# Hybrid encoder on one core: the roundings of the first part's operand sums one pair later, and the loads of the running sums spread over blocks 9 to 13

## The chip, the core and the metric

The kernel runs on one core of one Trainium2 chip. The metric is the device time of one execution, in microseconds: the median of the runs. The compute engines are PE (TensorE, matmuls, with PEld for its weight loads), DVE (VectorE), ACT (ScalarE) and POOL (GpSimd). DMAs are issued from the queues of SP (SyncE) and POOL.

## The reference, cut to what matters

Two layers (`DEPTH = 2`) on 512 tokens of width 1024, all in float32. Each layer mixes tokens in three ways, and then comes a SwiGLU feed-forward network (FFN), which the change is in:

```python
h = rmsnorm(x, norm_ffn[i])
x = x + (jax.nn.silu(h @ w_ffn_gate[i]) * (h @ w_ffn_up[i])) @ w_ffn_down[i]
```

`w_ffn_gate` and `w_ffn_up` are 1024 x 2816, `w_ffn_down` is 2816 x 1024. A per-layer input embedding follows, and a final norm behind the second layer.

## The kernel before, in words

**Operands in two halves.** A float32 operand is split in a high half (rounded to fp32r by ACT) and a low half (the difference, by DVE): `split`, lines 169 to 171, whose two instructions stand at lines 150 (ACT) and 164 (DVE) in the profile, as do all that go through the helpers `act` and `tt`. A product of two operands is three matmuls: high by high, high by low, low by high. In `seven` they are lines 1135, 1136 and 1137.

**The FFN in blocks and parts.** `ffn` walks over the 2816 inner columns in 22 blocks of 128, in three parts: blocks 0 to 7, 8 to 14 and 15 to 21 (`PARTS`). For each block `seven` computes gate and up together by a scheme of seven half-sized products in place of eight (of the Strassen kind): PE runs, in this order, a11·b11 into PSUM tile A, a22·t4 into Q, s2·t1 into C ("five"), a12·b21 onto A, s1·t3 onto Q, s3·t2 into A's other half, s4·b22 into C. Each is twelve matmuls of 128 x 256. The s are sums of weights, the t are sums of activations. Even blocks use the PSUM tags `mm`, odd blocks `sc`, `sc`, `av`.

ACT copies the products p1 (A, before a12·b21 is added onto it), p4 (Q, before s1·t3 is added) and p5 ("five") to SBUF; the products that add onto A and Q wait for these copies. p1 and p4 are the two halves of one tile of tag `t` (`ffn_t` in the profile), p5 is a tile of tag `a`. DVE then combines: p4 − p5, gate's two halves `gg` (scaled by the norm's factor `rb`), p1's difference, up's two halves `uu`. The first instruction that writes the tile `uu` is `uu0`, p1's difference minus Q.

**What follows a block.** `rest` (silu of `gg` on ACT, the product with `uu` on DVE, the split of the block's result into `md`) is kept in `self.pending`; `flush` runs it in the middle of the next block, right behind that block's copy of p5. At its end `rest` calls `done`.

**Pairs of blocks.** The first part's down product is again of the seven-product kind (`seven_down`, four calls, lines 1008 to 1088), in steps of pairs of blocks: (0, 1), (2, 3), (4, 5), with blocks 6 and 7 taken whole. It needs four sums t1 to t4 for each pair. `done` of the odd block calls `middles` (lines 996 to 1006), which makes them in two float32 tiles of tag `t` (DVE, 128 x 256 each) and right away splits each of them: four roundings on ACT, four low halves on DVE. The targets lie in tiles of tag `x`, in unused halves of `md`, and for the pair (2, 3) in tiles of the FFN's input.

**The running sums.** `seven_down` adds nothing to the residual: its eight results go to a DRAM buffer `xa` (line 1088, `xa<-ffn_t`) and come back as the tiles `x[m]` (line 1254, `ffn_x<-xa`), which the later parts' down products add to. Part 1 reads them first, behind block 14.

**Weights.** Each block loads its gate and up weights by four DMAs of SP (`ffn_qk<-w_fg`, `ffn_qk<-w_fu`, `ffn_wr<-w_fg`, `ffn_r<-w_fu`) and two accumulating ones of POOL; ACT rounds them and DVE makes their low halves and the sums s3 and s4. The order between the last: low half of a22 (`ffn_a<-ffn_r,ffn_kh`), then s3 (`ffn_qk<-ffn_qk,ffn_r`), then s4 (`ffn_qk<-ffn_qk,ffn_wr`), then the rounding of both (`ffn_pt` or `ffn_y`). `ffn_r` comes free when s3 is done.

**What sets the order.** PE's order is that of the code (`manual_schedule`). All other engines, and the queues of SP and POOL, are ordered by the framework's planner: it goes by priority, which is the place in the code (weights count as 400 instructions earlier, `w_ahead`), and places an instruction when its inputs are ready by its own durations. Buffers of a tag are handed out in the code order of first writes, so a tile's first write is not placed ahead of the first write of a tile of the same tag that comes earlier in the code: p1's copy of block n+1 not ahead of `uu0` of block n (tag `t`, seven buffers); the low half of a later block's a22 not ahead of the next block's copy of p5 (tag `a`, three buffers).

Of the kernel before, what the change touches and what calls it, by code (L numbers as in the profile page):

```python
# [26 lines left out]
KD = 8  # L27
# [41 lines left out]
class Net:  # L69
# [926 lines left out]
    def middles(self, at, even, odd):  # L996

        u, w = self.sb("t", [P, 2, 256]), self.sb("t", [P, 2, 256])
        t1, t2, t3, t4 = u[:, 0], u[:, 1], w[:, 0], w[:, 1]
        self.tt(t1, even[:, 0], even[:, 1], ALU.subtract)  # L1000
        self.tt(t2, odd[:, 1], t1, ALU.add)
        self.tt(t3, odd[:, 1], even[:, 1], ALU.subtract)
        self.tt(t4, odd[:, 0], t2, ALU.subtract)
        for (hi, lo), t in zip(at, (t1, t2, t3, t4)):
            self.split(hi, lo, t)
        return {f"t{n + 1}": t for n, t in enumerate(at)}

    def seven_down(self, p, w0, w1, bs, late, spare):

# [195 lines left out]
    def ffn(self, h, x):  # L1205
        self.phase = "ffn"
        i = self.i
        self.halfs, self.pending = 0, []
        nc, st, hn, bs = self.nc, [], [], self.four
        spare = [[self.sb(t, [P, 1024], F32R) for _ in range(2)] for t in ("pt", "y")]  # L1210
        md8 = [self.sb(t, [P, 2, 512], F32R) for t in ["v"] * 3 + ["z"] + ["y"] * 3]
        md8.append(tuple(self.sb("e", [P, 512], F32R) for _ in range(2)))
        low, xt = [], []
        for n in range(4):
            t = self.sb("x", [P, 2, 512], F32 if n == 2 else F32R)
            if n == 2:
                xg = t
            else:
                xt.append([(t[:, u, :256], t[:, u, 256:]) for u in range(2)])
        self.sums, self.sevens = [t for _ in range(2) for t in self.parts_of("qk", [1024], 2)], 0  # L1220
        for part in PARTS:
            mids = []
            for f, fb in enumerate(part):
                tags = (("mm", "mm", "mm"), ("sc", "sc", "av"))[fb % 2]
                md = md8[f]
                mids.append(md)
                wg, wu = self.a["w_fg"][i, fb], self.a["w_fu"][i, fb]
                gg = xg[:, fb // 2 % 2].rearrange("p (a b) -> p a b", a=2) if fb in (0, 2, 4) else None

                def done(gg, fb=fb):  # L1230
                    if fb > 5:
                        return
                    ha = self.halves(md8[fb - fb % 2])
                    cut = lambda p, c: (p[0][:, c], p[1][:, c])
                    one, two = slice(0, 256), slice(256, 512)
                    own = [cut(ha, two)]
                    if fb % 2 == 0:
                        self.even = gg
                    else:
                        hb = self.halves(md8[fb])  # L1240
                        at = (xt[0] + xt[1][:1] + own, [cut(self.halves(t), two) for t in h[::2]],
                              xt[1][1:] + xt[2] + own)[fb // 2]
                        low.append(dict(b11=cut(ha, one), b21=cut(hb, one), b22=cut(hb, two),
                                        **self.middles(at, self.even, gg)))

                self.seven(wg, wu, bs, tags, spare[fb % 2], md, part[0] and f < 2, fb, gg, done)
            self.flush()
            if part is PARTS[0]:
                for p in range(4):
                    w0, w1 = (self.a["w_fd"][i, 2 * p + u] for u in range(2))  # L1250
                    self.seven_down(p, w0, w1, low, mids[6:], spare[p % 2])
                x[:] = [t for _ in range(KD // 2) for t in self.parts_of("x", [512], 2)]
                for m in range(KD):
                    nc.sync.dma_start(x[m], self.xa[m])
                continue
            down = [self.a["w_fd"][i, m][:, part[0] * P:(part[-1] + 1) * P] for m in range(KD)]
            end = part is PARTS[-1]
            afresh = AFRESH[PARTS.index(part)]
            xs = [x[m] if m >= afresh else self.sb("a", [P, 512]) for m in range(KD) if end]
            for m in range(afresh if end else 0):  # L1260
                nc.sync.dma_start(xs[m], self.xp[m])
            two = [self.ps(("mm", "sc")[fb % 2 == 0]) for _ in range(2)]
            self.pair(two, down[:2], mids)
            for m in range(KD):
                if m < 2:
                    ps = two[m]
                else:
                    ps = self.ps("mm")
                    if m >= afresh:
                        self.act(ps, x[m], AF.Copy)  # L1270
                        if end:
                            nc.sync.dma_start(xs[m], self.xp[m])
                    self.gemm(ps, down[m], mids, m >= afresh)
                if not end and m >= afresh:
                    self.act(x[m], ps, AF.Copy)
                    continue
                if not end:
                    self.tt(x[m], x[m], ps, ALU.add)
                    continue
                d = self.sb("t", [P, 512])  # L1280
                if m < afresh:
                    self.tt(d, x[m], ps, ALU.add)
                    ps = d
                self.tt(d, ps, self.rb, ALU.mult)
                self.tt(x[m], xs[m], d, ALU.add)
                if m in (0, 2):
                    qk = self.parts_of("qk", [2, 512], 2, F32R)
                hn.append(self.norm_chunk(m, x[m], self.par(i, "ple", m),
                                          qk[m % 2] if m < 4 else "z", st))
        self.main_norm(st[0])  # L1290
        return hn
# [352 lines left out]
```

## Time and profile before

| | |
|---|---|
| median of 3 runs | 1772.17 us (1770.05 to 1772.83) |
| the profiled execution | 1771.02 us |
| its span in the profile | 1769.2 us |
| granted TensorE clock | 0.999 |
| DMA | 275.50 MB, 156 GB/s on average |
| the first part's blocks 3 to 7, layer 0 | 523.21 to 576.29 us |
| the first part's down product, layer 0 | 576.29 to 617.53 us |
| block 9, layer 0 | 627.57 to 638.46 us |

How to read it: a line of a timeline gives start and duration in microseconds, engine, line, operation, the tiles written and read (`out<-in`), and in brackets how long the engine stood before it and which instruction released it. `L150` and `L164` are the helpers, so instructions are told apart by their tiles. A tile's name is its phase and its tag: `ffn_t` is any tile of tag `t` in the FFN. A matmul's duration is longer than its distance to the next, as matmuls overlap; waits of PE are read from start to start. In a table of windows each engine has its busy time and, in brackets, its number of instructions.

### The profile page before, as it was taken

The numbers are of one execution on the slowest core, as the hardware profiler recorded it, in microseconds if no ns is written. First come the engines' busy times: TensorE is split into PE (matmuls) and PEld (weight loads), VectorE is DVE, ScalarE is ACT, GpSimd is POOL, SyncE is SP. The second block draws the span as 40 slices with busy tenths as digits, with TensorE's granted clock in tenths as the row PEclk, the third lists the DMA queues.
The fourth block names the chain that finished last, engine by engine and source line by source line (L and its number), as shares of the span: only waits on it lengthen the run. The fifth ranks groups of instructions, "written<-read, shape, count | busy, mean of one in ns | idle before, by whom it ended". The sixth has DMA issues, their size and how long they took to land.

```text
span 1769.2 us, 27985 instructions
## 1 busy us (share of the span) xinstructions
PE 1756.1 (99%) x10362; PEld 1559.0 (88%) x10362; DVE 1430.5 (81%) x2434; ACT 915.7 (52%) x1599; POOL 112.3 (6%) x130
## 2 busy tenths in 40 slices
PE   9999999999999999999999999999999999999998
PEld 7888888888899999998888888888888999989987
DVE  7967988998899886687777688889887997866776
ACT  5576555325566454454545665552356554534454
POOL 0000000000111111100000000000001111101000
PEclk9999999999999999999999999999999999999999
DMA  6576641334867886545546755323358678755342
GB/s 227 161 187 158 160 125 54 102 99 151 258 164 168 225 220 160 136 124 163 164 135 171 184 151 153 106 76 92 107 182 236 167 166 241 211 143 152 99 152 95
DMA packets 127529, 275.50 MB, mean 156 GB/s; under 512 B 16032, under 2 KB 31136, under 8 KB 127392
## 3 DMA queue, kind: packets, MB, share of 16 engines
q1 hardware_dynamic: 111696, 246.19, 45.7%
q0 software_dynamic: 14976, 26.22, 9.3%
q8 instruction: 81, 1.33, 0.3%
q10 hardware_dynamic: 720, 1.31, 0.2%
q14 instruction: 56, 0.46, 0.1%
HBM read 227.52 MB, written 15.73 MB: 137 GB/s over the span
## 4 chain that ended last, share of the span: by engine, by line
PE 92%; DVE 3%; DMA 2%; ACT 2%; issue 1%; POOL 0%; SPq 0%; ACTq 0%; POOLq 0%; DVEq 0%
PE ffn_mm L1135 4%; PE ffn_mm L1137 4%; PE ffn_mm L1136 4%; PE ffn_sc L1137 3%; PE ffn_sc L1135 3%; PE ffn_sc L1136 3%; PE ffn_mm L185 3%; PE ffn_mm L186 3%; PE ffn_mm L187 3%; PE mergea_mm L185 2%; PE mergea_mm L187 2%; PE mergea_mm L186 2%; PE gateb_mm L187 2%; PE gateb_mm L186 2%; PE gateb_mm L185 2%; PE wo_mm L187 2%
## 5 line engine op out<-in xcount | busy, mean ns | idle before, releaser
L167 DVE SCALAR_TENSOR_TENSOR conv_z<-glu_z,pre_par,conv_z 128x512 f32<-128x512 f32 x240 | 179.4, 747 | 3.5
L150 ACT ACTIVATE ffn_wh<-ffn_wr 128x1024 fp32r<-128x1024 f32 (+1 forms) x84 | 84.5, 1010 | 63.4 <-PE ffn_mm L186 32.4
L164 DVE TENSOR_TENSOR ffn_wl<-ffn_wr,ffn_wh 128x1024 fp32r<-128x1024 f32 (+1 forms) x84 | 97.8, 1169 | 21.3 <-ACT ffn_wh L150 20.8
L1105 POOL DMA_DIRECT2D ffn_qk<-w_fu x88 | 77.9, 980 | 525.6 <-DMA ffn_qk<-w_fu 236.2
L150 ACT ACTIVATE ffn_wh<-ffn_qk 128x1024 fp32r<-128x1024 f32 x52 | 55.1, 1060 | 44.4 <-PE ffn_mm L1061 17.8
L164 DVE TENSOR_TENSOR ffn_wl<-ffn_qk,ffn_wh 128x1024 fp32r<-128x1024 f32 x52 | 63.6, 1223 | 16.9 <-ACT ffn_wh L150 16.6
L150 ACT ACTIVATE mergea_wh<-mergea_wr 128x1024 fp32r<-128x1024 f32 (+1 forms) x32 | 27.1, 846 | 96.8 <-PE mergea_mm L186 79.6
L164 DVE TENSOR_TENSOR ffn_t<-ffn_t,ffn_t 128x512 f32<-128x512 f32 (+1 forms) x58 | 34.6, 596 | 25.4 <-ACT ffn_t L150 24.8
L150 ACT ACTIVATE ffn_kh<-ffn_r 128x512 fp32r<-128x512 f32 (+1 forms) x52 | 31.9, 613 | 42.1 <-DMA ffn_r<-w_fu 12.7
L150 ACT ACTIVATE natten_e<-natten_e,natten_s 128x192 f32<-128x192 f32 (+1 forms) x88 | 39.3, 473 | 25.1 <-DVE natten_s L732 21.8
L1135 PE MATMUL ffn_sc<-wo_h,ffn_wh 128*128 128x256 f32 x176 | 50.0, 284 | 1.5 <-ACT ffn_t L150 1.5
L150 ACT ACTIVATE diff_a<-diff_sc,diff_s 128x512 f32<-128x512 f32 x32 | 22.0, 686 | 56.8 <-DVE diff_s L925 56.7
L1137 PE MATMUL ffn_mm<-wo_h,ffn_wl 128*128 128x256 f32 x176 | 49.8, 283 | 0.0
L1136 PE MATMUL ffn_mm<-wo_h,ffn_wh 128*128 128x256 f32 x176 | 49.8, 283 | 0.0
L1136 PE MATMUL ffn_sc<-wo_h,ffn_wh 128*128 128x256 f32 x176 | 49.8, 283 | 0.0
L1135 PE MATMUL ffn_mm<-wo_h,ffn_wh 128*128 128x256 f32 x176 | 49.8, 283 | 0.0
L1137 PE MATMUL ffn_sc<-wo_h,ffn_wl 128*128 128x256 f32 x176 | 49.8, 283 | 0.0
L231 POOL TENSOR_TENSOR diff_rc<-diff_sm,pre_power 128x4 f32<-128x4 f32 x8 | 8.9, 1115 | 563.0 <-DVE diff_sm L167 504.4
L164 DVE TENSOR_TENSOR diff_wl<-diff_wr,diff_wh 128x1024 fp32r<-128x1024 f32 x24 | 29.3, 1223 | 18.7 <-ACT diff_wh L150 13.6
L150 ACT ACTIVATE natten_wh<-natten_wr 128x1024 fp32r<-128x1024 f32 x24 | 25.4, 1059 | 36.7 <-issue 15.2
L925 DVE TENSOR_REDUCE diff_s<-diff_sc 128x1 f32<-128x512 f32 x64 | 42.0, 682 | 2.2 <-PE diff_sc L834 2.1
L164 DVE TENSOR_TENSOR natten_wl<-natten_wr,natten_wh 128x1024 fp32r<-128x1024 f32 x24 | 29.3, 1222 | 12.3 <-ACT natten_wh L150 10.4
(1086 smaller groups left out, 6817.3 us busy)
## 6 DMA issues: line engine op xcount, KB each, us to landing
ffn_qk<-w_fu POOLq DMA_DIRECT2D x88, 256.0 KB, 6.1
ffn_wr<-w_fg SPq DMA_DIRECT2D x44, 512.0 KB, 5.1
ffn_wr<-w_fd SPq DMA_DIRECT2D x32, 448.0 KB, 4.0
ffn_r<-w_fu SPq DMA_DIRECT2D x44, 256.0 KB, 3.8
ffn_qk<-w_fg SPq DMA_DIRECT2D x44, 256.0 KB, 5.3
ffn_qk<-w_fu SPq DMA_DIRECT2D x44, 256.0 KB, 5.4
natten_wr<-w_in SPq DMA_DIRECT2D x16, 512.0 KB, 4.4
diff_wr<-w_in SPq DMA_DIRECT2D x16, 512.0 KB, 4.0
```

What stands on the lines that cost most here:

```text
L150: i = self.nc.scalar.activation(out, in_, func, **kw)
L164: return self.nc.vector.tensor_tensor(out, a, b, op)
L167: return self.nc.vector.scalar_tensor_tensor(out, a, s, b, op0, op1)
L185: mm(out, wh, ah, start=first, stop=False, skip_group_check=onto)
L186: mm(out, wh, al, start=False, stop=False, skip_group_check=onto)
L187: mm(out, wl, ah, start=False, stop=last, skip_group_check=onto)
L231: nc.gpsimd.tensor_tensor(col, ms, self.power, ALU.pow)
L925: nc.vector.tensor_reduce(out=m[:, u:u + 1], in_=sc, op=ALU.max, axis=AX.X, negate=True)
L1105: nc.gpsimd.dma_start(q, wu[:, lo], accum_op=ALU.add)
L1135: mm(out, wh[:, c], bh, start=first and k == 0, stop=False, skip_group_check=True)
L1136: mm(out, wh[:, c], bl, start=False, stop=False, skip_group_check=True)
L1137: mm(out, wl[:, c], bh, start=False, stop=k == 3, skip_group_check=True)
```

## The change

`middles` no longer splits the four sums. It puts target and sum in a list, `self.parted`, and a new method `part_sums` splits all that the list holds. `done` of an even block calls it: so the sums of pair (0, 1), made in `done` of block 1, are split in `done` of block 2, those of pair (2, 3) in `done` of block 4, those of pair (4, 5) in `done` of block 6 (for blocks 6 and 7 `done` does nothing else). In the code each group of splits thus comes one block later, and the two tiles of sums are held a block longer.

The eight loads of the running sums no longer stand together behind the first part. They stand ahead of blocks of the second part: sum 0 ahead of block 9, 1 ahead of 10, 2 and 3 ahead of 11, 4 and 5 ahead of 12, 6 and 7 ahead of 13. The number of instructions is the same.

```diff
@@ middles @@
-        for (hi, lo), t in zip(at, (t1, t2, t3, t4)):
+        self.parted += zip(at, (t1, t2, t3, t4))
+        return {f"t{n + 1}": t for n, t in enumerate(at)}
+
+    def part_sums(self):
+
+        for (hi, lo), t in self.parted:
             self.split(hi, lo, t)
-        return {f"t{n + 1}": t for n, t in enumerate(at)}
+        self.parted = []
@@ ffn @@
-        low, xt = [], []
+        low, xt, self.parted = [], [], []
...
             for f, fb in enumerate(part):
+                for m in {9: (0,), 10: (1,), 11: (2, 3), 12: (4, 5), 13: (6, 7)}.get(fb, ()):
+                    nc.sync.dma_start(x[m], self.xa[m])
...
                 def done(gg, fb=fb):
                     if fb > 5:
-                        return
+                        return self.part_sums()
...
                     if fb % 2 == 0:
+                        self.part_sums()
                         self.even = gg
...
                 x[:] = [t for _ in range(KD // 2) for t in self.parts_of("x", [512], 2)]
-                for m in range(KD):
-                    nc.sync.dma_start(x[m], self.xa[m])
                 continue
```

## The prediction

> **What bounds the kernel now.** I read the page first, then the waits of PE, then PE's timeline at each wait, the windows of the blocks around it, and last the timelines of ACT, DVE and SP in those windows.
>
> ```profile
> span 1769.2 us, 27985 instructions
> PE 1756.1 (99%) x10362; PEld 1559.0 (88%) x10362; DVE 1430.5 (81%) x2434; ACT 915.7 (52%) x1599; POOL 112.3 (6%) x130
> ```
>
> TensorE is busy for 1756.1 of 1769.2 us. The change takes no matmul away, so all it can give is time in which PE stands. PE's waits, and the matmuls that end three of them, in the first layer:
>
> ```profile
> PE ffn_av L1135 <- ACT ffn_t L150: 3.9, 4, 1.6
> PE ffn_sc L1135 <- ACT ffn_t L150: 1.5, 2, 0.7
> ```
> ```profile
> 528.42 0.39 PE L1135 MATMUL ffn_sc<-wo_h,ffn_wh 128*128 128x256 f32 x1 [0.75 <-ACT ffn_t L150]
> 531.73 0.38 PE L1135 MATMUL ffn_av<-wo_v,ffn_wh 128*128 128x256 f32 x1 [1.62 <-ACT ffn_t L150]
> 634.06 0.39 PE L1135 MATMUL ffn_av<-wo_v,ffn_wh 128*128 128x256 f32 x1 [0.60 <-ACT ffn_t L150]
> ```
>
> The two largest waits are PE waiting for ACT to copy p1 and p4 out of PSUM, in block 3 (528.42, 531.73) and block 9 (634.06). The windows show each block whole; the columns are length, then busy time of PE, PEld, DVE, ACT, POOL, clock, DMA share and GB/s. The first five are blocks 3 to 7 of layer 0, then block 9, then blocks 3 and 9 of layer 1.
>
> ```profile
> 523.21:536.13 12.92, 10.55 (x86) 10.15 (x85) 12.91 (x26) 6.90 (x14) 1.76 (x2) 1.00 0.73 200
> 536.13:546.17 10.04, 10.04 (x86) 10.04 (x85) 8.71 (x17) 5.98 (x10) 1.76 (x2) 1.00 0.71 173
> 546.17:556.22 10.05, 10.05 (x87) 10.05 (x86) 9.96 (x20) 6.24 (x11) 1.75 (x2) 1.00 0.69 156
> 556.22:566.25 10.03, 10.03 (x86) 10.03 (x85) 9.97 (x19) 6.19 (x11) 1.79 (x2) 1.00 0.71 175
> 566.25:576.29 10.04, 10.04 (x86) 10.04 (x85) 10.01 (x22) 5.87 (x11) 1.72 (x2) 1.00 0.68 155
> 627.57:638.46 10.89, 10.29 (x87) 10.09 (x86) 7.28 (x14) 5.45 (x9) 1.78 (x2) 1.00 0.78 235
> 1398.93:1411.70 12.77, 10.56 (x86) 10.16 (x85) 12.76 (x26) 6.63 (x13) 1.75 (x2) 1.00 0.67 189
> 1503.14:1513.67 10.53, 10.32 (x86) 10.12 (x85) 7.30 (x14) 5.45 (x9) 1.75 (x2) 1.00 0.79 229
> ```
>
> An undisturbed block lasts 10.04. Block 3 costs 2.88 and 2.73 over that in the two layers, 5.61 together; block 9 costs 0.85 and 0.49, together 1.34. Those 6.95 us are the most that the change can give. In block 3 DVE has no gap (12.91 of 12.92) and in blocks 5 to 7 hardly one; in block 4 it has 1.33 idle.
>
> **Part 1, the low halves of the sums.** ACT in block 3, then in block 5, which has no stall:
>
> ```profile
> 527.70 0.38 ACT L150 ACTIVATE ffn_a<-ffn_sc 128x256 f32<-128x256 f32 x1 [0.62 <-PE ffn_sc L1137]
> 527.98 0.38 ACT L150 ACTIVATE ffn_t<-ffn_sc 128x256 f32<-128x256 f32 x1
> 530.35 1.06 ACT L150 ACTIVATE ffn_pt<-ffn_qk 128x1024 fp32r<-128x1024 f32 x1 [1.99 <-DVE ffn_qk L164]
> 531.32 0.36 ACT L150 ACTIVATE ffn_t<-ffn_av 128x256 f32<-128x256 f32 x1
> ```
> ```profile
> 549.66 0.36 ACT L150 ACTIVATE ffn_t<-ffn_sc 128x256 f32<-128x256 f32 x1
> 550.67 0.38 ACT L150 ACTIVATE ffn_a<-ffn_sc 128x256 f32<-128x256 f32 x1 [0.38 <-PE ffn_sc L1137]
> ```
>
> In block 5 ACT copies p1 (549.66), then p4, then p5 (550.67). In block 3 the order is p5, p1, the rounding of s3 and s4 (`ffn_pt`), p4; both waits follow from it. ACT idles 0.62 ahead of p5, so p1 is not late for lack of ACT: its place in the queue is wrong. The planner hands out a tag's buffers in code order of first write, so p1's buffer of block n+1 comes behind `uu` of block n, which DVE writes first in `uu0` (p1 minus Q). If DVE reaches `uu0` only when p5 is ready, p5 goes first. So: `uu0` must start before p5 of the next block.
>
> What holds `uu0` up in block 3 is four low halves of the sums (columns: start, duration), while the `uu0` of blocks 3 to 6, which run in blocks 4 to 7, stand here with them:
>
> ```profile
> 526.03 1.09 DVE L164 TENSOR_TENSOR ffn_x<-ffn_t,ffn_x 128x256 fp32r<-128x256 f32 x3
> 527.04 0.42 DVE L164 TENSOR_TENSOR ffn_v<-ffn_t,ffn_v 128x256 fp32r<-128x256 f32 x1
> 537.07 0.42 DVE L164 TENSOR_TENSOR ffn_t<-ffn_t,ffn_av 128x256 f32<-128x256 f32 x1
> 550.19 0.42 DVE L164 TENSOR_TENSOR ffn_t<-ffn_t,ffn_mm 128x256 f32<-128x256 f32 x1
> 558.94 0.42 DVE L164 TENSOR_TENSOR ffn_t<-ffn_t,ffn_av 128x256 f32<-128x256 f32 x1
> 570.61 0.42 DVE L164 TENSOR_TENSOR ffn_t<-ffn_t,ffn_mm 128x256 f32<-128x256 f32 x1
> ```
>
> Three low halves take 526.03 to 527.04, 0.336 each from start to start; four take 1.35. Behind them stand p4−p5, a product and p1's difference at the same step, three more, so `uu0` of block 2 could start at 526.03 + 3 × 0.336 = 527.04 instead of behind s3 and s4, 0.66 ahead of p5 at 527.70. Then p1 and p4 are copied first, as in block 5, and both waits go: −5.61 over the two layers. The low halves and ACT's four roundings are not saved, only moved; ACT is half idle (6.90 of 12.92) and hides its share at no cost, but if DVE's cover is gone each low half costs up to 0.336.
>
> What is late next? Without the stall DVE loses 2.88 us per layer in which it caught up. Its work in blocks 3 to 7 is 12.91 + 8.71 + 9.96 + 9.97 + 10.01 = 51.56, less 1.36 of the last pair's low halves, which move behind block 7: 50.2, in 5 × 10.04 = 50.2. No slack. I carry the debt on. p5 is copied 4.50 into a block (550.67 − 546.17).
> - Block 4: `uu0` at 537.07 − 536.13 = 0.94, plus 2.88 of debt (the first pair's low halves now lie ahead of it): 3.82, margin 0.68.
> - Block 5: the debt falls by block 4's 1.33 to 1.55, and this pair's 1.36 lies behind: 4.02 + 0.19 = 4.21, margin 0.29.
> - Block 6: 558.94 − 556.22 = 2.72, plus 1.55: 4.27, margin 0.23.
> - Block 7: 570.61 − 566.25 = 4.36, plus 0.19: 4.55, 0.05 too late; but the next low half of the weights (tag `a`, as p5) is handed its buffer only behind p5, so DVE has nothing to put ahead of `uu0`, and p1 slips by one copy at most.
>
> So a slip in block 7 costs the first of block 3's two waits, 0.75, not the second. The next step is the down product; ACT's row gives what a 128x512 tile takes there.
>
> ```profile
> 578.10 0.28 PE L1049 MATMUL ffn_tr<-ffn_x,ffn_pt 128*128 128x256 f32 x1
> 584.39 0.41 PE L1061 MATMUL ffn_mm<-ffn_e,ffn_wh 128*128 128x512 f32 x1
> ```
> ```profile
> 576.83 0.68 DVE L164 TENSOR_TENSOR ffn_t<-ffn_t,ffn_t 128x512 f32<-128x512 f32 x1
> 579.82 0.42 DVE L164 TENSOR_TENSOR ffn_t<-ffn_t,wo_rb 128x256 f32<-128x256 f32 x1
> 580.89 0.42 DVE L164 TENSOR_TENSOR ffn_a<-ffn_tr,ffn_t 128x256 f32<-128x256 f32 x1 [0.65 <-PE ffn_tr L1051]
> 583.56 0.68 DVE L164 TENSOR_TENSOR ffn_e<-ffn_t,ffn_e 128x512 fp32r<-128x512 f32 x1
> ```
> ```profile
> 633.11 0.63 ACT L150 ACTIVATE ffn_kh<-ffn_r 128x512 fp32r<-128x512 f32 x1 [3.52 <-DMA ffn_r<-w_fu]
> ```
>
> Block 7's own low half ends at 583.56 + 0.68 = 584.24, 0.15 ahead of its use at 584.39; PE will be there 2.88 sooner, at 581.51. Block 7's last result ends at 579.82 + 0.42 = 580.24; DVE can make up at most block 4's 1.33 and some 0.19 in the gaps of blocks 5 to 7, so that becomes 578.72 or later. From there silu, product, rounding and low half take between 2.62 (0.63 + 0.68 + 0.63 + 0.68, back to back) and 4.00 (as now): 581.34 to 582.72. PE waits between nothing and 1.21. I take 0.6, the middle, because both ends have DVE rows behind them (the 0.65 idle at 580.24 can be filled): +1.2 for two layers. A slip in block 7 hands its 0.75 to DVE and takes the place of this wait, so the two are not added.
>
> **Part 2, the loads of the running sums.** SP at the last stores, the release of the buffer that its next load needs, and what waits:
>
> ```profile
> 588.83 0.33 SPq L1254 DMA_DIRECT2D ffn_x<-xa  x1
> 619.26 0.92 SPq L1088 DMA_DIRECT2D xa<-ffn_t  x2
> 624.84 1.11 SPq L1254 DMA_DIRECT2D ffn_x<-xa  x2
> 626.06 0.44 SPq L1103 DMA_DIRECT2D ffn_r<-w_fu  x1
> ```
> ```profile
> 620.35 0.68 DVE L164 TENSOR_TENSOR ffn_qk<-ffn_qk,ffn_r 128x512 f32<-128x512 f32 x1
> ```
> ```profile
> 771.67 0.33 SPq L842 DMA_DIRECT2D diff_r<-rope  x1
> ```
>
> SP stands until the stores of 619.26 have landed (5.58), loads the last two sums at 624.84, and only then issues `ffn_r` at 626.06, whose buffer was free at 621.03. `ffn_r` lands before 633.11 (the ACT row above); ACT stands 3.52 for it with p4's copy behind it, and that is block 9's wait. The change writes these loads later in the code. But the planner issues a load when its inputs and buffer are ready: the rope tables of layer 1 went at 771.67, before half of the span (884.6), about where layer 1 begins, and the first sum at 588.83, right after its store. The two last loads stay where they become ready, so I count nothing. If `ffn_r` does pass them it comes up to 5 us sooner (626.06 − 621.03) and the whole 1.34 goes. A loss is left out: the sums are first read in part 1's down product, five blocks on. Ends: 0 and −1.34; I take 0.
>
> By the Trainium skill ("DMA: Bandwidth & Descriptors", section "Anatomy of one DMA"), whose fit stands for the GpSimd path, a transfer takes about 2.0 us plus its bytes over 436 GB/s, most of the fixed part being the receipt of the write. An estimate by it for one 256 KB store is 2.6 us, so SP would be free some 3 us sooner and block 9 would not wait at all; the trace has 5.58, so it does not agree here, and by the page part 2 would be worth nothing even if the loads moved.
>
> **Sum.** −5.61 + 1.2 + 0 = −4.4: 1766.6 for the profiled execution (1771.02), and, as that lies 1.15 below the median of 1772.17, 1767.8 for the median. A measurement of this kernel tells from no change about 0.2%, 3.5 us.
>
> **Rivals.**
> - Both parts work: −5.61 + 1.2 − 1.34 = −5.75, 1766.4; without the wait for block 7's low half −6.95, 1765.2. For it: `ffn_r` stands in the queue behind loads that nobody needs before part 1's down product. Against it: 771.67. Chance 0.15.
> - The stall only moves or shrinks. With margins of 0.2 to 0.7, a few tenths of difference between the planner's durations and the trace's turn the order again in one of blocks 4 to 7, with up to 2.88 per layer: nothing left. Or block 3 keeps its order and only the second wait shrinks by 1.35: −2.7, 1769.5. Between 1769 and 1772.5; chance 0.26.
> - The change does nothing: the planner fills DVE as before and leaves the low halves where they were: 1772.2. Against it: they now rank behind block 2's results. Chance 0.06.
> - Slower: the last pair's low halves come too late. The down product reads the second of them at 578.10, in the new time 575.2; the product of block 6 at 576.83 ranks ahead of them and becomes 574.1 (1.36 + 1.36 earlier); two low halves behind it end at about 575.5, some 0.1 late, which is within the 0.6 taken above. From there each 0.1 us costs 0.2 over two layers; above 2.8 late the gain is used up. Behind block 7's last result (580.24 − 2.7 + 0.8 = 578.3) they are 3.1 late, +0.6, 1772.8; behind its low half (584.24) 7.1 late, +8.6, 1780.8. Against it: by rank they stand ahead of all of block 7's results. Chance 0.11, of which 0.07 is slower by over 0.2%.
>
> **How the numbers follow.** The forecast has 0.42. Of it 0.36 lies beyond 3.5 us of gain, the rest (a wait at its upper end) within; with the first rival faster has 0.51. Within 0.2%: 0.06 + 0.26 + 0.06 + 0.04 = 0.42; slower 0.07. The range goes from 1765.2 to 1772.8, which leaves out the slow end and the executions' own scatter.
>
> **What would show it.** In the changed profile: block 3 at 10.04 in both layers with p1, p4, p5 in ACT's queue in that order (right), or p5 first again (wrong); the first pair's four low halves behind `uu0` of block 2; no block of 4 to 7 above 10.1 except block 7 by up to 0.75; a wait of PE L1061 for DVE `ffn_e` of 0 to 1.2; block 9 still 10.89 and 10.53, with the last loads of sums issued ahead of `ffn_r`. The forecast is wrong if one of blocks 4 to 7 shows a wait above 1 us, if L1049 waits for `ffn_x`, or if block 9 falls to 10.04.

## The result, and the profile after

The changed kernel takes 1764.93 us (median of 6 runs, 1763.43 to 1765.64), the kernel before, timed beside it, 1771.58 (6 runs, 1769.46 to 1772.83): a ratio of 0.9963, with a 95% interval of 0.9950 to 0.9976, so 6.65 us less (4.3 to 8.9). The forecast was 1767.8, from 1765.2 to 1772.8: the sign is right, and the median lies 0.27 us below the lower end. The page of the changed kernel:

```profile
span 1763.0 us, 27985 instructions
PE 1754.5 (100%) x10362; PEld 1557.8 (88%) x10362; DVE 1429.8 (81%) x2434; ACT 915.8 (52%) x1599; POOL 112.4 (6%) x130
```

Its profiled execution took 1764.80. The waits of PE (line numbers from `seven` on are five higher than before), then the windows of blocks 3, 4, 7 and 9 of layer 0 and of blocks 3 and 9 of layer 1, then the down product of layer 0:

```profile
PE ffn_av L1140 <- ACT ffn_t L150: 1.4, 2, 0.8
```
```profile
522.22:532.26 10.04, 10.04 (x86) 10.04 (x85) 10.04 (x20) 6.55 (x13) 1.77 (x2) 1.00 0.72 192
532.26:542.30 10.04, 10.04 (x86) 10.04 (x85) 10.01 (x19) 5.46 (x9) 1.77 (x2) 1.00 0.70 169
562.38:572.42 10.04, 10.04 (x86) 10.04 (x85) 10.04 (x22) 6.58 (x13) 1.72 (x2) 1.00 0.66 181
623.84:634.66 10.82, 10.28 (x86) 10.08 (x85) 7.27 (x14) 5.45 (x9) 1.78 (x2) 1.00 0.79 226
1395.14:1405.18 10.04, 10.04 (x86) 10.04 (x85) 9.96 (x20) 6.27 (x12) 1.75 (x2) 1.00 0.68 181
1496.75:1507.88 11.13, 10.30 (x87) 10.10 (x86) 7.29 (x14) 5.45 (x9) 1.75 (x2) 1.00 0.76 220
```
```profile
572.42:613.80 41.38, 41.38 (x303) 39.17 (x301) 33.52 (x60) 17.04 (x22) 7.05 (x8) 1.00 0.81 223
```

Block 3 lasts 10.04 in both layers: its 2.88 and 2.73 are gone. The wait on p1 (`ffn_sc`) has left the list, and of the wait on p4 (`ffn_av`) only block 9's is left. Blocks 4 to 7 are at 10.04, with DVE full in each (10.01 to 10.04). No wait for the last pair's sums (`ffn_x`) is in the list: of their four low halves the last two run at 573.42 and 573.76, in time. Block 9 still waits, in layer 1 even more (11.13). ACT in block 3:

```profile
526.01 0.37 ACT L150 ACTIVATE ffn_t<-ffn_sc 128x256 f32<-128x256 f32 x1
526.27 0.38 ACT L150 ACTIVATE ffn_t<-ffn_av 128x256 f32<-128x256 f32 x1
526.72 0.39 ACT L150 ACTIVATE ffn_a<-ffn_sc 128x256 f32<-128x256 f32 x1
```

p1, p4, p5: the order of the blocks without a stall.

### The profile page after: what moved, and what is told of

The parts are those of the page before. It is cut to its first block, busy times and chain, and to the rows that moved or that the text cites. A ratio compares the mean times of both kernels' runs of the same rounds, so it can differ in the third digit from the quotient of the medians.

```text
span 1763.0 us, 27985 instructions
## 1 busy us (share of the span) xinstructions
PE 1754.5 (100%) x10362; PEld 1557.8 (88%) x10362; DVE 1429.8 (81%) x2434; ACT 915.8 (52%) x1599; POOL 112.4 (6%) x130
## 3 DMA queue, kind: packets, MB, share of 16 engines
q8 instruction: 81, 1.33, 0.3%
## 4 chain that ended last, share of the span: by engine, by line
PE 97%; DMA 1%; ACT 1%; DVE 1%; issue 0%; POOL 0%; ACTq 0%; POOLq 0%; DVEq 0%
PE ffn_mm L1140 4%; PE ffn_mm L1142 4%; PE ffn_mm L1141 4%; PE ffn_sc L1142 3%; PE ffn_sc L1140 3%; PE ffn_sc L1141 3%; PE ffn_mm L187 3%; PE ffn_mm L186 3%; PE ffn_mm L185 3%; PE mergea_mm L187 2%; PE mergea_mm L186 2%; PE mergea_mm L185 2%; PE diff_sc L834 2%; PE diff_mm L185 2%; PE diff_mm L187 2%; PE gatec_mm L186 2%
```

## The experiments

The theory: PE waited because p1 stood behind p5, and p4 behind the rounding of s3 and s4 too, in ACT's queue, and they stood there because DVE came to `uu0` too late. The rival: the time that DVE (or ACT) spends on the split is itself what PE waited for, so that any work moved out of block 3 gives its time. Beside them, the loads of the running sums may have given a part.

Each run is one edit to the kernel before or after. The runs of the kernel before that stand beside them have medians of 1770.22 to 1770.87 (19 to 25 runs), so runs of different sets are compared by their ratios to them.

**The roundings and low halves alone** (the kernel after, with the loads back where they were).

```diff
-                for m in {9: (0,), 10: (1,), 11: (2, 3), 12: (4, 5), 13: (6, 7)}.get(fb, ()):
-                    nc.sync.dma_start(x[m], self.xa[m])
...
+                for m in range(KD):
+                    nc.sync.dma_start(x[m], self.xa[m])
```

> Only the roundings and low halves of the sums move; the loads of the running sums stay in one place behind the first part. If the whole gain comes from block 3 (the order of ACT's copies), this is as fast as the full change: 1765 us, block 3 at 10.04 in both layers, block 9 still above 10.4. If the loads gave part of the gain (the measured 6.65 us are more than the 5.4 that block 3 lost between the two traces), this is slower than the full change: 1766 or more, with the difference in block 9 or behind it.

Measured: 1765.22, ratio 0.9969 (0.9958 to 0.9981), which can't be told from the full change. Block 3 is at 10.04 in both layers.

```profile
523.95:533.99 10.04, 10.04 (x87) 10.04 (x85) 10.04 (x20) 6.55 (x13) 1.76 (x2) 1.00 0.77 213
```

Within the intervals the whole gain comes from this part. Block 9 fell to 10.47 and 10.04 without its loads having moved, the first sign that its wait scatters.

**The loads alone** (the opposite edit, to the kernel before).

> Only the loads of the running sums move in the code. If the planner issues a load when it is ready, SP's order and everything else is that of the kernel before: 1771.6 us within 0.1%, block 3 at 12.9 and 12.8, block 9 within its scatter. If the place in the code counts, ffn_r passes the loads and block 9 falls to 10.04: 1.3 us less, 1770.2.

Measured: 1770.72, ratio 1.0001 (0.9992 to 1.0010). SP issues the last loads between the stores and `ffn_r`, as before; every engine and every queue has the order of the kernel before, instruction by instruction:

```profile
619.83 0.92 SPq L1088 DMA_DIRECT2D xa<-ffn_t  x2
624.88 0.93 SPq L1225 DMA_DIRECT2D ffn_x<-xa  x2
625.91 0.44 SPq L1103 DMA_DIRECT2D ffn_r<-w_fu  x1
```

Moving these eight loads in the code as the change does has no effect.

**p1 and p4 in a tag of their own** (to the kernel before; the low halves stay where they were).

```diff
-        o = self.sb("t", [P, 2, 256])
+        o = self.sb("o", [P, 2, 256], bufs=2)
...
-        self.bufs = dict(wr=3, wh=3, wl=3, h=8, qk=2, kh=2, v=4, pt=2, y=5, z=5, x=4, t=7, rp=4,
-                         e=4, a=3, r=2, rb=1, ss=1, sm=8, rc=4, b=2, s=8)
+        self.bufs = dict(wr=3, wh=3, wl=3, h=8, qk=2, kh=2, v=4, pt=2, y=5, z=5, x=4, t=6, rp=4,
+                         e=4, a=3, r=2, rb=1, ss=1, sm=8, rc=3, b=2, s=8)
```

> The kernel before, with the low halves where they were, but p1 and p4 in a tag of their own (two buffers; tag t has six in place of seven and a small tag three in place of four), so that their place in ACT's queue no longer hangs on uu0. If the order of ACT's copies is the cause, block 3 falls to 10.04 in both layers though the four low halves still stand ahead of uu0, and the time is 1766 (5.4 less). If the time that DVE spends on the low halves is the cause by itself, block 3 stays at 12.9 and the time at 1771.6. With one buffer of tag t less, another wait may appear elsewhere; then block 3 alone decides.

Measured: 1766.29, ratio 0.9977 (0.9967 to 0.9987), with block 3 at 10.04 in both layers. Block 3 of both layers, then ACT's copies and DVE's low halves and `uu0` in it:

```profile
524.33:534.37 10.04, 10.04 (x87) 10.04 (x86) 10.04 (x19) 5.85 (x11) 1.77 (x2) 1.00 0.75 179
1396.81:1406.85 10.04, 10.04 (x86) 10.04 (x85) 10.04 (x19) 5.86 (x11) 1.76 (x2) 1.00 0.61 171
```
```profile
525.97 0.38 ACT L150 ACTIVATE ffn_o<-ffn_sc 128x256 f32<-128x256 f32 x1 [1.51 <-PE ffn_sc L1137]
527.95 0.37 ACT L150 ACTIVATE ffn_o<-ffn_av 128x256 f32<-128x256 f32 x1
528.83 0.38 ACT L150 ACTIVATE ffn_a<-ffn_sc 128x256 f32<-128x256 f32 x1 [0.51 <-PE ffn_sc L1137]
```
```profile
526.99 1.08 DVE L164 TENSOR_TENSOR ffn_x<-ffn_t,ffn_x 128x256 fp32r<-128x256 f32 x3
531.13 0.41 DVE L164 TENSOR_TENSOR ffn_t<-ffn_o,ffn_mm 128x256 f32<-128x256 f32 x1
```

This is the run that decides between the two theories: the low halves stand where they stood, `uu0` comes at 531.13, 2.3 us behind p5, and PE does not wait, because p1 (525.97) and p4 no longer hang on it. What PE waited for was the place of two copies in ACT's queue; DVE's time mattered only in that the planner placed p1 by it. About 1 us is lost elsewhere: block 0 lasts 11.39 and 11.38 against 10.89 and 10.88 before, and in it `wo_tr` waits for POOL's `wo_rc`, whose tag has one buffer less (0.6 in total).

**The last loads behind `ffn_r`** (to the kernel after).

```diff
-            nc.sync.dma_start(a22, wu[:, up])
+            self.rl[fb] = nc.sync.dma_start(a22, wu[:, up])
...
-                    nc.sync.dma_start(x[m], self.xa[m])
+                    load = nc.sync.dma_start(x[m], self.xa[m])
+                    if m > 5:
+                        self.behind(load, self.rl[11])
```

> The full change, and the last two loads of running sums are put behind the ffn_r of block 11 in SP's queue. If those loads held ffn_r up (SP stood 5.6 us for the stores, its buffer was free after 1.8), ffn_r is issued some 3 to 4 us sooner, block 9 falls from 10.9 and 11.0 to 10.04 in the two layers and the time by 1.8 us, to 1763. If the transfer itself is late whatever its place (7.8 us from its issue to ACT's rounding), block 9 keeps half of its wait or more: 1764 to 1765.

Measured: 1764.35, ratio 0.9964 (0.9952 to 0.9977). SP after the last stores, first of the change, then of this run, and block 9 of both layers in this run:

```profile
615.52 0.93 SPq L1093 DMA_DIRECT2D xa<-ffn_t  x2
620.50 0.91 SPq L1230 DMA_DIRECT2D ffn_x<-xa  x2
621.52 0.44 SPq L1108 DMA_DIRECT2D ffn_r<-w_fu  x1
```
```profile
616.87 0.92 SPq L1093 DMA_DIRECT2D xa<-ffn_t  x2
618.70 0.33 SPq L1108 DMA_DIRECT2D ffn_r<-w_fu  x1
```
```profile
625.18:635.22 10.04, 10.04 (x87) 10.04 (x85) 8.08 (x15) 5.67 (x9) 1.78 (x2) 1.00 0.82 236
1497.35:1507.39 10.04, 10.04 (x86) 10.04 (x85) 8.08 (x15) 5.67 (x9) 1.76 (x2) 1.00 0.91 223
```

`ffn_r` is issued 1.83 behind the stores in place of 6.00, and block 9 is at 10.04 in both layers. That the new order brought this is not shown: in the eleven profiles with the old order in SP's queue, 7 of the 22 blocks 9 have no wait to speak of (0.05 or less) either, in the run with p1 and p4 in a tag of their own those of both layers. The time does not fall by the 1.8 expected; it can't be told from the change's. With the old order block 9's wait is 0.85 and 0.49 in the kernel before, 0.43 and nothing with the low halves alone, nothing and 1.52 in the run that follows, on average over the eleven profiles some 0.9 for both layers together: that is what there is to gain, and it is below what these runs resolve.

**Only the first pair later** (to the kernel after, with the loads back where they were; the other pairs are split at once).

```diff
-    def middles(self, at, even, odd):
+    def middles(self, at, even, odd, low):
...
         self.parted += zip(at, (t1, t2, t3, t4))
+        if len(low):
+            self.part_sums()
```

> Only pair (0, 1) is split a block later; pairs (2, 3) and (4, 5) are split at once, as before, and the loads stand where they were. If what counts is where uu0 stands against p5 in each block, block 3 falls to 10.04, and the stall comes back in block 5, where pair (2, 3)'s low halves still stand ahead of uu0 and DVE now carries a debt of some 1.3 us: 0.75 to 2.9 per layer, so 1766.5 to 1770.5. If only the low halves in block 3 matter, this is as fast as moving all three pairs: 1765, and no block from 4 to 7 is longer than 10.1.

Measured: 1771.14, ratio 1.0004 (0.9994 to 1.0013): nothing is gained. Blocks 3 and 5 of layer 0 (block 5 of layer 1 lasts 13.27), and ACT in block 5:

```profile
523.24:533.28 10.04, 10.04 (x86) 10.04 (x85) 10.04 (x20) 6.54 (x13) 1.77 (x2) 1.00 0.73 179
543.32:556.32 13.00, 10.57 (x86) 10.16 (x85) 12.98 (x27) 7.37 (x14) 1.76 (x2) 1.00 0.65 180
```
```profile
547.82 0.38 ACT L150 ACTIVATE ffn_a<-ffn_sc 128x256 f32<-128x256 f32 x1 [0.61 <-PE ffn_sc L1144]
548.10 0.38 ACT L150 ACTIVATE ffn_t<-ffn_sc 128x256 f32<-128x256 f32 x1
550.53 1.06 ACT L150 ACTIVATE ffn_pt<-ffn_qk 128x1024 fp32r<-128x1024 f32 x1 [2.05 <-DVE ffn_qk L164]
551.49 0.37 ACT L150 ACTIVATE ffn_t<-ffn_av 128x256 f32<-128x256 f32 x1
```

The stall has moved to block 5, line for line the picture of block 3 before: p5, p1, the rounding of s3 and s4, p4. The stall, 2.96 and 3.23, is a little above the range expected. Moving block 3's low halves is not enough; the later pairs must move as well.

**Roundings at once, low halves later** (all pairs, to the kernel after with the loads back where they were; one run).

```diff
+        for (hi, lo), t in self.parted:
+            self.act(hi, t, AF.Copy)
...
-            self.split(hi, lo, t)
+            self.tt(lo, t, hi.bitcast(F32), ALU.subtract)
```

> All three pairs: ACT rounds the sums at once, as before, and only DVE's low halves come a block later; the loads stand where they were. If DVE's place in time is all that counts, as fast as the full change: 1765, block 3 at 10.04. If ACT's four roundings (0.4 us each) also hold p1 or p4 up, block 3 keeps a wait of some tenths.

Measured: 1765.43, block 3 at 10.04 in both layers. ACT's roundings play no part in block 3's stall; a single time says no more.

**The first pair's low halves twice** (to the kernel after: the same result is written a second time).

```diff
             self.split(hi, lo, t)
+            if self.more:
+                self.tt(lo, t, hi.bitcast(F32), ALU.subtract)
+        self.more = self.more and not self.parted
```

`self.more` is true at the start of each `ffn`, so only the first group of sums is written twice.

> The full change, with each low half of pair (0, 1) computed twice: 4 times 0.336 = 1.35 us more for DVE per layer, in block 4 ahead of uu0 of block 3. That uu0 started 3.74 into block 4 with p5 at 4.50, so the margin of 0.76 is exceeded. If the order theory holds, p5 goes first in block 4, and PE waits there for p1 and perhaps p4: 0.75 to 2.9 per layer, 1766.4 to 1770.7. If DVE's total work is what counts, block 4 stays at 10.04 and the 1.35 arrive at the low half of block 7's result in the down product: 0.7 to 1.3 per layer there, 1766.4 to 1767.6.

Measured: 1770.16, ratio 0.9998 (0.9988 to 1.0007). Block 4 of layer 0 (in layer 1 it lasts 12.74):

```profile
533.52:546.23 12.71, 10.54 (x86) 10.14 (x85) 12.71 (x25) 6.15 (x10) 1.77 (x2) 1.00 0.76 207
```

1.35 us of DVE work bring 2.7 us of stall back in each layer, in the block whose margin they exceed.

**One low half twice** (to the kernel after).

```diff
-        for (hi, lo), t in self.parted:
+        for n, ((hi, lo), t) in enumerate(self.parted):
             self.split(hi, lo, t)
+            if self.more and n < 1:
+                self.tt(lo, t, hi.bitcast(F32), ALU.subtract)
+        self.more = self.more and not self.parted
```

> The full change, with only one low half of pair (0, 1) computed twice: 0.336 us more for DVE per layer. In the full change uu0 of block 3 started 3.74 into block 4 and uu0 of block 4 started 4.22 into block 5, with p5 at 4.50. If the margins decide, block 4 keeps its order (3.74 + 0.34 = 4.08) and block 5 loses it (4.22 + 0.34 = 4.56): p5 goes first there and PE waits 2.5 to 3 us per layer, so one instruction of 0.42 us in each layer costs 5 to 6 us: 1770 to 1771. If the time lost grows with the work added, it costs at most 0.34 per layer, 1765.6.

Measured: 1766.69, ratio 0.9978 (0.9968 to 0.9987). By the ratios that is 1.6 us above the low halves alone and 2.7 above the change, less than the intervals can tell; the traces give 1.01 per layer. Blocks 4 and 5 of layer 0, then ACT in block 5:

```profile
533.45:543.49 10.04, 10.04 (x87) 10.04 (x85) 10.01 (x20) 5.58 (x9) 1.76 (x2) 1.00 0.74 197
543.49:554.54 11.05, 10.30 (x87) 10.10 (x86) 11.05 (x22) 6.90 (x13) 1.75 (x2) 1.00 0.71 194
```
```profile
547.99 0.38 ACT L150 ACTIVATE ffn_a<-ffn_sc 128x256 f32<-128x256 f32 x1 [0.61 <-PE ffn_sc L1145]
548.27 0.38 ACT L150 ACTIVATE ffn_t<-ffn_sc 128x256 f32<-128x256 f32 x1
548.53 0.39 ACT L150 ACTIVATE ffn_t<-ffn_av 128x256 f32<-128x256 f32 x1
```

The place was right, block 5 and not block 4, and one instruction of 0.42 us costs 1.01 in each layer (block 5 of layer 1 is 11.05 too). The price was wrong, 2.5 to 3 were expected: a narrow miss puts only p5 ahead of p1, and p4 keeps its place, so only the first of the two waits comes back.

**The first pair's low halves twice, with the own tag** (both edits shown above, to the kernel after).

> All four low halves of pair (0, 1) twice (1.35 us more per layer, as in the run that brought the stall back in block 4), and p1 and p4 in a tag of their own, so that their place in ACT's queue does not hang on uu0. If the stall in block 4 was the order, blocks 4 and 5 stay at 10.04 and only the debt is paid, at the low half of block 7's result in the down product: 0.9 to 1.35 per layer; with the 1.1 that the own tag's smaller buffers cost beside, 1768 to 1769. If DVE's added work makes the stall by itself, block 4 waits 2.6 per layer again and the time is 1770 or more.

Measured: 1768.39, ratio 0.9987 (0.9978 to 0.9997). Block 4 and the down product:

```profile
534.25:544.29 10.04, 10.04 (x86) 10.04 (x85) 10.04 (x20) 5.00 (x8) 1.76 (x2) 1.00 0.72 190
574.41:617.45 43.04, 41.75 (x302) 39.16 (x301) 35.20 (x66) 17.57 (x23) 7.07 (x8) 1.00 0.80 219
```

Blocks 4 to 7 stay at 10.04; the debt is paid once, in the down product: 43.04 against 41.50 with the own tag alone, 1.54 (43.06 and 1.56 in layer 1) and so a little above the range expected, which ended at 1.35. The 0.2 between is not explained. The stall of the run without the own tag was the order.

**The last pair's low halves twice** (to the kernel after).

```diff
             self.split(hi, lo, t)
+            if self.last:
+                self.tt(lo, t, hi.bitcast(F32), ALU.subtract)
...
+                        self.last = True
                         return self.part_sums()
```

> The full change, with each low half of pair (4, 5) computed twice: 1.35 us more for DVE per layer, behind block 7's uu0 test, so the order of ACT's copies stays. In the changed kernel the low half of block 7's result ended at 580.51, with its use at about 580.5: no margin. The extra 1.35 then reach it, less what the chain behind block 7's last result has in pauses (3.28 used against 2.62 back to back): a wait of 0.7 to 1.35 per layer at the whole products of the down product, 1766.3 to 1767.6. If that low half still has slack of its own, nothing: 1765.

Measured: 1767.86, ratio 0.9983 (0.9974 to 0.9992). The whole products of the down product, and its window:

```profile
581.10 0.49 PE L1067 MATMUL ffn_mm<-ffn_e,ffn_wh 128*128 128x512 f32 x1 [0.39 <-ACT ffn_e L150]
581.84 0.50 PE L1068 MATMUL ffn_mm<-ffn_e,ffn_wh 128*128 128x512 f32 x1 [0.24 <-DVE ffn_e L164]
```
```profile
572.36:615.07 42.71, 42.01 (x303) 39.21 (x302) 34.86 (x64) 17.05 (x22) 7.09 (x8) 1.00 0.80 215
```

The down product lasts 42.71 in place of 41.38, in layer 1 42.73 in place of 41.37: 1.35 us more on DVE bring 1.33 and 1.36 on PE, and the time lies 0.3 above the range expected. The next wait is where the prediction put it, and in the changed kernel its margin is nothing.

## Why the prediction was wrong in size

**Block 3: right.** "−5.61 over the two layers" is what the two traces show: 12.92 and 12.77 became 10.04 and 10.04, by the order p1, p4, p5, and the own tag shows that the order is the cause. One detail was not right: the prediction put all four low halves behind `uu0`. One of the four still runs ahead of it, in both layers (here layer 0):

```profile
526.05 0.41 DVE L164 TENSOR_TENSOR ffn_x<-ffn_t,ffn_x 128x256 fp32r<-128x256 f32 x1
526.38 0.41 DVE L164 TENSOR_TENSOR ffn_t<-ffn_t,ffn_mm 128x256 f32<-128x256 f32 x1
```

So `uu0` comes 0.34 ahead of p5 (526.72), and not the 0.66 forecast.

**The carried debt: no block slipped, but one of the agreements is luck.** `uu0` in blocks 4 to 7 of the changed kernel, and the low half ahead of block 5's:

```profile
536.00 0.42 DVE L164 TENSOR_TENSOR ffn_t<-ffn_t,ffn_av 128x256 f32<-128x256 f32 x1
546.19 0.41 DVE L164 TENSOR_TENSOR wo_h<-ffn_t,wo_h 128x256 fp32r<-128x256 f32 x1
546.52 0.41 DVE L164 TENSOR_TENSOR ffn_t<-ffn_t,ffn_mm 128x256 f32<-128x256 f32 x1
556.13 0.42 DVE L164 TENSOR_TENSOR ffn_t<-ffn_t,ffn_av 128x256 f32<-128x256 f32 x1
566.60 0.41 DVE L164 TENSOR_TENSOR ffn_t<-ffn_t,ffn_mm 128x256 f32<-128x256 f32 x1
```

Less the blocks' starts (532.26, 542.30, 552.34, 562.38) `uu0` comes at 3.74, 4.22, 3.79 and 4.22; forecast were 3.82, 4.21, 4.27 and 4.55. The first two are met; the last two were put 0.48 and 0.33 too late, as 1.82 and 2.02 of the debt had been made up by then, and no block slipped. In block 5 two errors cancel. Here too one of the pair's low halves stays ahead of `uu0` (546.19, `wo_h<-ffn_t,wo_h`), so three lie behind, 1.00 and not 1.36; and of the debt 1.68 had been made up, not 1.33. The sums are 2.68 and 2.69. p5 is copied 4.50 into blocks 4 and 5, which leaves margins of 0.76 and 0.28. The runs with one and four low halves more agree with these: each broke the order in the block in which its addition exceeds the margin. The planner goes by its own durations, which no view shows, so that the trace's margins hold to a tenth is not shown.

**The step that failed: "DVE can make up at most block 4's 1.33 and some 0.19 in the gaps of blocks 5 to 7, so that becomes 578.72 or later", and with it the term "+1.2 for two layers".** The last result of block 7 and the low half behind it, in the changed kernel, then the matmul that needs it:

```profile
576.81 0.42 DVE L164 TENSOR_TENSOR ffn_t<-ffn_t,wo_rb 128x256 f32<-128x256 f32 x1
579.82 0.69 DVE L164 TENSOR_TENSOR ffn_e<-ffn_t,ffn_e 128x512 fp32r<-128x512 f32 x1
```
```profile
580.56 0.50 PE L1066 MATMUL ffn_mm<-ffn_e,ffn_wh 128*128 128x512 f32 x1
```

From block 3's start to that result's start DVE now takes 576.81 − 522.22 = 54.59, before 579.82 − 523.21 = 56.61: of 2.88 it made up 2.02, not 1.52. The result ends at 577.23; this execution runs 0.99 early (its block 3 starts at 522.22), so in the prediction's time 578.22, half a microsecond sooner than "578.72 or later". The chain from there to the end of the low half took 580.51 − 577.23 = 3.28, the middle of the 2.62 to 4.00 forecast. The low half ends at 580.51, the matmul starts at 580.56, and the down product is 41.38 long against 41.24: 0.14, and 0.13 in layer 1 (41.37 against 41.24). The term is +0.27, not +1.2.

The half microsecond was in the trace. The idle time had been read from the window (10.04 − 8.71 = 1.33), which counts from the end of one instruction to the start of the next. The kernel before in block 4:

```profile
538.41 0.42 DVE L164 TENSOR_TENSOR ffn_t<-ffn_x 128x256 f32<-128x256 f32 x1
539.32 0.42 DVE L164 TENSOR_TENSOR wo_h<-ffn_t,wo_h 128x256 fp32r<-128x256 f32 x1 [0.48 <-ACT wo_h L150]
```

DVE's instructions of this size follow each other at 0.335, though each is recorded as 0.42 (with 512 columns at 0.60, recorded as 0.68). So here 0.91 − 0.335 = 0.58 is lost, where the bracket says 0.48. From start to start block 4 has 1.55 to give, and eight pauses of 0.09 to 0.14 between block 3's start and block 7's last result give another 0.90. Both kernels run 107 instructions of the same shapes there; of these 2.45 the changed one keeps 0.43, so 2.02 are made up. The Trainium skill ("VectorE: DVE Perf Modes", section "The DRAIN you can't avoid") says that a next instruction waits until the pipeline has emptied, but that one that is not held starts earlier. The trace's 0.335 against 0.42 agrees with the second, if the recorded end is taken for that of the pipeline, which no run here shows.

**Part 2: right.** No order changed and no time (1.0001). The Trainium skill's fit for the GpSimd path ("DMA: Bandwidth & Descriptors", section "Anatomy of one DMA"), by which SP would stand 2.6 us (an estimate), is not met here either: 4.98 from the stores to the load in the change (615.52 to 620.50).

**The rest of the distance.** The forecast for the profiled execution was 1766.6, measured are 1764.80, 1.8 less. The term above accounts for 0.93 of it. Block 9 took 0.53 more than before (10.82 and 11.13 against 10.89 and 10.53), in the other direction. 0.99 had gone before block 3, in code that is the same in both kernels, and 0.42 lie behind the last matmul. In the ten profiles that have the same code up to the FFN, block 3 starts between 522.15 and 523.95: such a start is scatter. The range's lower end held no such scatter, since it was drawn at "the most that the change can give"; that is the second mistake. The runs of the low halves alone, 0.9969 with 21 runs of the kernel before beside them, put the gain at 5.5 us (3.4 to 7.4), and 5.61 − 0.27 = 5.34 from the trace fits. The "1.15" by which the forecast was raised for the median was scatter too: it came from a median of 3 runs, 1772.17, and the larger sets put the kernel before at 1770.22 to 1770.87, near the profiled execution's 1771.02. The forecast gain of 4.4 by itself lies within the measured interval (4.3 to 8.9), at its edge; that 1.2 was too much is known from the traces, and not from the times.

## What to carry to other kernels

Where a planner orders the queues, a wait can come from where an instruction was placed and not from how long anything takes: look for an engine that idles right ahead of the instruction that is late, and ask what decided the order. Such an order breaks at a margin, so make a table of the margins in all blocks before work is moved, and check afterwards that each margin was met for the reason given; here a single instruction of 0.42 us more cost 1 us per layer. And count what a full engine can make up from start to start, not from the idle time of a window.

## What the runs showed of the hardware that I had not expected

With the same order in SP's queue, the wait for one 256 KB load (`ffn_r`, behind two other loads) cost block 9 between nothing and 1.52 us, and differently in the two layers of one execution. Nor does the time of its issue foretell the cost: issued 9.60 behind the start of block 8 (kernel before, layer 1) it cost 0.49, issued 7.72 behind it (kernel after, layer 0) 0.79. One profile shows what a wait cost in one execution; a wait that ends with a DMA needs several.
